# Weight-quarter differences moved from GpSimd to VectorE, squaring moved to ScalarE, tiles placed at multiples of 512 bytes, in a two-layer encoder on one core

## The chip, the cores and the metric

The kernel runs on one core of one Trainium2 chip. The metric is device time in microseconds (us) of one execution. The median of a few runs is compared, before and after the change, on the same chip. One further execution was recorded by the hardware profiler; all rows below are of it. Engine names follow the profile: PE is TensorE's matmul, PEld its weight load, DVE is VectorE, ACT is ScalarE, POOL is GpSimd, SP is the queue that issues the DMAs.

## The reference, cut to what matters

Two layers over 512 tokens of 1024 channels, all in float32. A layer projects its input, runs three attention branches (A with 4 heads, B with 8 query heads, C with 4 heads), gates and merges them, projects, normalizes, and then runs an MLP:

```python
for layer in range(DEPTH):                     # DEPTH = 2
    h = x @ w_in[layer]                        # q, k, v of three branches, gate logits
    oa, ob, oc = ...                           # the three attentions, 512 x 512 scores a head
    merged = g0 * (oa @ w_branch_a) + g1 * (ob @ w_branch_b) + g2 * (oc @ w_branch_c)
    x = layer_norm(ALPHA * x + merged @ w_out[layer])
    ff = jnp.square(jax.nn.relu(x @ w_up[layer])) @ w_down[layer]   # 1024 -> 4096 -> 1024
    x = layer_norm(ALPHA * x + ff)
```

## The kernel before

**Products.** Each float32 operand is split into a high and a low part of the fast float32 format, and each product is three matmuls, high by high, high by low and low by high (`mm3`, lines 152 to 155). A weight tile of 128 x 1024 arrives by DMA as `raw` (or `braw`), ACT copies it into `whi` (line 182), and DVE subtracts to give `wlo` (line 183). Eight split tiles are in flight: five in the pool `wts`, three in a second weight pool that exists outside of attention. PE frees them one after another, and a tile that is freed lets the next split start.

**Stages of a layer.** Projections and three attentions run interleaved (matmuls into `psq`, `psc`, `psg`, `psb`, `pss`, `pso`, transposes into `psp`, `psk`); then a tail of branch B's gates (`psg`, 24 matmuls) and branch products (`psb`, 12 matmuls) for eight column blocks m; then the output projection with its layer norm, and the MLP. The MLP runs in four quarters q of 1024 hidden channels.

**A quarter of the MLP.** Eight blocks m go through PE into `psu` (24 matmuls each). After each block `hidden(m, ps)` runs: ACT takes Relu out of the bank into half of a tile `f` (line 910), DVE squares it in place (line 911), and the result is split into `hh` on ACT (line 231) and `hl` on DVE (line 232). In quarters 0 to 2 the down projection is a seven-product scheme for 2 x 2 blocks (the class `Fast`), so `hidden` also makes sums and differences of the squares: after an odd m, line 918 (`f[:,4] = f[:,0] + f[:,2]`) and line 921 (three differences), all on DVE, 128 x 256 each. Slot 0 of `hh` and `hl` is split after an even m, slots 1 to 3 and 4 to 6 after an odd m.

**A `Fast` pass.** Seven steps of 24 matmuls each into `psd`. The first step takes slot 0 of all four pairs of blocks, the pair of m = 6 and 7 last (matmuls 10 to 12 of the first bank). The weights of a step are a quarter of the down matrix or a difference of quarters. `operand(i, half)` makes it: six tiles `braw` are loaded for a pass and two more at step 5, and for four of the seven steps (i = 1, 2, 4, 6) a tile is overwritten by the difference of two, once for each half:

```python
if a is not None:
    nc.gpsimd.tensor_tensor(dst, a, b, op=ALU.subtract)      # line 796, 128 x 1024
```

That is 8 differences in a pass and 48 in the kernel. Each reads tiles that were split shortly before, and is split itself next.

**The first quarter of a layer** is cut in token halves for its first four blocks (line 925), so their four banks are done about 2.9 us apart, where the other blocks are 5.45 us apart. Quarter 3 uses a plain down projection without differences.

**Order.** A tile scheduler orders each engine's queue when the program is built. Within an engine, instructions run in that order, each waiting for its own semaphores.

**Placement.** Pools lie one behind the other in each partition's memory, and their tiles are multiples of 64 bytes. In the built program `raw`, `whi`, `wlo` of `wts`, `xTh` and `xTl` (the transposed input) start 192 bytes past a multiple of 512, the second weight pool 448 past, the tiles of attention 320 or 64 past (`oh` and `ol`, the attention outputs that `psb` multiplies: 320), and the MLP's tiles 192 past.

Of the kernel before, what the change touches and what calls it, by code (L numbers as in the profile page):

```python
# [11 lines left out]
F32 = mybir.dt.float32  # L12
F32R = mybir.dt.float32r
AF = mybir.ActivationFunctionType
ALU = mybir.AluOpType
AX = mybir.AxisListType

P = 128
# [4 lines left out]
KB = D // P  # L23
# [13 lines left out]
C_OFF = {0: 0, 1: 256, 2: 640, 3: 1024}  # L37
C_WID = 1280
LINE = 16


class Split:
# [86 lines left out]
def encoder(ctx: ExitStack, tc: tile.TileContext, x, x_t, w_qkv, w_c, w_gate, b_gate, qn, kn, rpb,  # L129
            w_ba, w_bb, w_bc, w_out, ln1_g, ln1_b, w_up, w_down, w_fast, ln2_g, ln2_b,  # L130
            mask_a, rope_a, rope_b, out):
    nc = tc.nc
    const = ctx.enter_context(tc.tile_pool(name="const", bufs=1))
# [1 line left out]
    glob = ctx.enter_context(tc.tile_pool(name="glob", bufs=1))  # L135
    dram = ctx.enter_context(tc.tile_pool(name="dram", bufs=1, space=bass.MemoryType.DRAM))
    edge = ctx.enter_context(tc.tile_pool(name="edge", bufs=1, side="right"))
    edge.tile([P, LINE // 2], F32, name="edge")
    psum = ctx.enter_context(tc.tile_pool(name="psum", bufs=8, space=bass.MemoryType.PSUM))

    def bank(name):
        return psum.tile([P, 512], F32, tag="ps", name=name)

    def f32(ap):
        return ap.bitcast(F32)

    ident = const.tile([P, P], F32, name="ident")
    make_identity(nc, ident)
    nhalf = const.tile([P, 16], F32, name="nhalf")
    nc.vector.memset(nhalf, -0.5)  # L150

    def mm3(ps, lhs, rhs, start, stop, again=False):
# [110 lines left out]
    def layer_norm(pool, z, st, gb, after=None):  # L263

        mv = pool.tile([P, LINE], F32, tag="mv", name="mv", bufs=4)[:, :2]
        nc.vector.bn_aggr(mv, st.rearrange("p a b -> p (a b)"))
        ve = pool.tile([P, LINE], F32, tag="ve", name="ve", bufs=4)[:, :2]
        nc.vector.tensor_scalar(ve[:, :1], mv[:, 1:2], LN_EPS, None, op0=ALU.add)
# [7 lines left out]
    def stats_tile(pool):  # L276
        return pool.tile([P, LINE], F32, tag="st", name="st", bufs=4)[:, :12].rearrange("p (a b) -> p a b", a=2)

# [19 lines left out]
    def attention(l, keep, qk, open_heads):  # L298
# [72 lines left out]
        def norm_rotate(tb):  # L371

            raw = raws["b"][:, tb]
            r = raw.rearrange("p (h d) -> p h d", d=HD)
            sq = pool.tile([P, 10, HD], F32, tag="sq", name="sq", bufs=2)
            nc.scalar.activation(sq, r, AF.Square)
            cs = pool.tile([P, 2, 2, HD], F32, tag="cs", name="cs", bufs=1)
            nc.vector.tensor_tensor(cs, gqk, ropeb[:, :, tb][:, None].to_broadcast([P, 2, 2, HD]), op=ALU.mult)
            yield 1
            ss = pool.tile([P, 2, LINE], F32, tag="ss", name="ss", bufs=2)[:, :, :10]  # L380
            nc.vector.tensor_reduce(ss[:, 0], sq, axis=AX.X, op=ALU.add)
            nc.vector.tensor_scalar(ss[:, 0], ss[:, 0], 1.0 / HD, RMS_EPS, op0=ALU.mult, op1=ALU.add)
            nc.gpsimd.tensor_tensor(ss[:, 1], ss[:, 0], nhalf[:, :10], op=ALU.pow)
            yield 2
            nc.vector.tensor_tensor(r, r, ss[:, 1][:, :, None].to_broadcast([P, 10, HD]), op=ALU.mult)
            t2 = pool.tile([P, 10, HD], F32, tag="sq", name="t2", bufs=2)
            spans = ((0, 8), (8, 10))
            for i, (h0, h1) in enumerate(spans):
                r4, t4 = (t[:, h0:h1].rearrange("p h (a b d) -> p h a b d", a=2, b=2) for t in (r, t2))
                sin = cs[:, i, 1].rearrange("p (a b d) -> p a b d", a=2, b=2)  # L390
                for b in range(2):
                    nc.gpsimd.tensor_tensor(t4[:, :, :, b], r4[:, :, :, 1 - b],
                                            sin[:, None, :, b].to_broadcast([P, h1 - h0, 2, 16]), op=ALU.mult)
            yield 2
            for i, (h0, h1) in enumerate(spans):
                nc.vector.tensor_tensor(r[:, h0:h1], r[:, h0:h1],
                                        cs[:, i, 0][:, None, :].to_broadcast([P, h1 - h0, HD]), op=ALU.mult)
            nc.vector.tensor_tensor(r, r, t2, op=ALU.add)
            if tb == TB - 1:
                flags.add("b")  # L400
# [106 lines left out]
        def keys_of(name, qb):  # L507
            return C_KEYS[qb] if name == "c" else (0, TB)

        def scores(name, h, qb):  # L510
            ks, qs = pairs[name, h // 2]
            q, k = qs[h % 2], ks[h % 2]
            k0, k1 = keys_of(name, qb)
            n = (k1 - k0) * P
            ps = bank("pss")[:, :n]
            nc.tensor.matmul(ps, q[:, qb * P:(qb + 1) * P], k.hi[:, k0 * P:k1 * P], start=True, stop=False)
            nc.tensor.matmul(ps, q[:, qb * P:(qb + 1) * P], k.lo[:, k0 * P:k1 * P], start=False, stop=True)
            p = pool.tile([P, S], F32, tag="p", name="p", bufs=4)[:, :n]
            st = pool.tile([P, LINE], F32, tag="stat", name="stat", bufs=4)
            if name == "b":  # L520
                s = ps
                nc.vector.tensor_reduce(st[:, 0:1], ps, axis=AX.X, op=ALU.max)
            else:
                s = p
                add = maska[:, (3 - qb) * P:(3 - qb) * P + S] if name == "a" else bias[h][:, C_OFF[qb]:C_OFF[qb] + n]
                nc.vector.tensor_tensor_reduce(s, ps, add, 1.0, -3e38, ALU.add, ALU.max, st[:, 0:1])
            nc.vector.tensor_scalar(st[:, 1:2], st[:, 0:1], -1.0, None, op0=ALU.mult)
            nc.scalar.activation(p, s, AF.Exp, bias=st[:, 1:2], accum_out=st[:, 2:3])

            def normalize():  # L530
                nc.vector.reciprocal(st[:, 3:4], st[:, 2:3])  # L531
                (nc.vector if name == "c" else nc.gpsimd).tensor_scalar(p, p, st[:, 3:4], 1.0, op0=ALU.mult, op1=ALU.mult)  # L532

            return p, normalize
# [115 lines left out]
        with tc.manual_schedule() if l == 0 else nullcontext():  # L650
            work.flush()
        pool = open_heads()
        hb = keep.tile([P, 4 * KB], F32, tag="hb", name="hb")[:, :3 * KB]
        nc.sync.dma_start(hb, b_gate[l])
        nc.vector.tensor_scalar(hb, hb, 0.5, None, op0=ALU.mult)
        gqk = pool.tile([P, 2, 2, HD], F32, tag="gqk", name="gqk", bufs=1)
# [108 lines left out]
    class Fast:  # L765
# [18 lines left out]
        def operand(self, i, half):  # L784

            if i == 0 and half == 0:
                for quarter in (0, 1, 3):
                    for h in range(2):
                        self.load(quarter, h, quarter)
            if i == 5:  # L790
                self.load(2, half, 1)
            b11, b12, b22 = (self.b[k, half] for k in (0, 1, 3))
            dst, a, b = ((b11, None, None), (b11, b12, b11), (b11, b22, b11), (b22, None, None),
                         (b12, b22, b12), (b12, None, None), (b11, b12, b11))[i]
            if a is not None:
                nc.gpsimd.tensor_tensor(dst, a, b, op=ALU.subtract)  # L796
            return dst

        def items(self):
# [37 lines left out]
    for l in range(L):  # L837
        with ExitStack() as left:
            def pool(stack, name, side="left"):
                return stack.enter_context(tc.tile_pool(name=f"{name}{l}", bufs=1, side=side, reuse_waits="tile"))  # L840

            keep = pool(left, "keep")
            with ExitStack() as inner:
                def open_heads():
                    right.close()
                    return pool(inner, "heads")
# [15 lines left out]
            with ExitStack() as inner:  # L862
# [12 lines left out]
                st = [stats_tile(mix) for _ in range(TB)]  # L875
# [22 lines left out]
            for q in range(4):  # L898
                hid, sums = [], []

                def hidden(m, ps):

                    if m % 2 == 0:
                        hid.append(mlp.tile([P, 8, 256], F32, tag="f", name="f"))
                        sums.append(Split(mlp.tile([P, 7, 256], F32R, tag=f"hh{m}", name="hh"),
                                          mlp.tile([P, 7, 256], F32R, tag=f"hl{m}", name="hl")))
                    f, h = hid[-1], sums[-1]
                    a = 2 * (m % 2)
                    r = f[:, a:a + 2]
                    nc.scalar.activation(r, ps.rearrange("p (a n) -> p a n", a=2), AF.Relu)  # L910
                    nc.vector.tensor_tensor(r, r, r, op=ALU.mult)
                    if q == 3:
                        split_psum(h.map(lambda t: t[:, a:a + 2]), r)
                    elif a == 0:
                        split_psum(h.map(lambda t: t[:, 0]), f[:, 1])
                    else:

                        nc.vector.tensor_tensor(f[:, 4], f[:, 0], f[:, 2], op=ALU.add)  # L918
                        split_psum(h.map(lambda t: t[:, 1:4]), f[:, 2:5])
                        for dst, x1, x2 in ((5, 4, 1), (6, 1, 0), (7, 3, 5)):  # L920
                            nc.vector.tensor_tensor(f[:, dst], f[:, x1], f[:, x2], op=ALU.subtract)
                        split_psum(h.map(lambda t: t[:, 4:7]), f[:, 5:8])
# [25 lines left out]
                st = [stats_tile(mlp) for _ in range(TB)]  # L948
# [133 lines left out]
```

## Time and profile before

| | us |
|---|---|
| median of 3 runs (lowest, highest) | 1533.81 (1532.96, 1535.28) |
| the profiled execution | 1538.57 |
| its span, first to last instruction | 1536.8 |
| PE busy | 1501.1 |
| DVE busy | 1096.1 |
| ACT busy | 688.0 |
| POOL busy | 311.6 |

Busy times are sums over the span of the profiled execution. A matmul's record is longer than the step from one matmul to the next, since matmuls are pipelined: for speed, the starts of successive matmuls are to be compared. In a timeline row, the columns are the start, the length, engine, line, operation, output and inputs with their shape, and the count; brackets hold the idle time of the engine just before and what ended it. Overlapping neighbours on one engine by up to 0.1 us are its pipeline.

### The profile page before, as it was taken

The page shows a single profiled execution, that of the slowest core. Times are in us where ns is not written, and L with a number is a line of the kernel's source. Part 1 is how long each engine was busy: PE and PEld are TensorE (multiplying, and loading weights), DVE is VectorE, ACT ScalarE, POOL GpSimd, SP SyncE. Part 2 cuts the span into 40 slices and gives each one's busy share as a digit, 9 for nine tenths or more (in the row PEclk, how much of TensorE's full clock was granted, in tenths as well). Part 3 has the DMA queues.
Part 4 walks back from the last instruction along what each step waited for, and adds up shares of the span by engine and source line. Part 5 has one row for each costly group of instructions (what it writes and reads, how often), then busy time and mean ns, then how long its engine had stood idle before and what let it go on. Part 6 is the DMA issues. An engine that isn't in the chain of part 4 may idle for free.

```text
span 1536.8 us, 19258 instructions
## 1 busy us (share of the span) xinstructions
PE 1501.1 (98%) x7256; PEld 1255.7 (82%) x7256; DVE 1096.1 (71%) x1722; ACT 688.0 (45%) x1096; POOL 311.6 (20%) x238
## 2 busy tenths in 40 slices
PE   7999999999998999999999999999999989999997
PEld 6888888888896888888888888888888968888886
DVE  4677977745588797964666787876447888979636
ACT  4565656533134343433236556565332343535320
POOL 0112212311142222210101141233111413222001
PEclk9999999999998999999999999999999999999999
DMA  6222321143242415042331323112441342340411
GB/s 218 84 79 70 112 68 53 58 164 118 75 178 81 139 56 164 1 131 85 114 129 56 99 77 110 55 55 76 160 133 56 152 137 83 91 129 28 138 55 55
DMA packets 43438, 150.63 MB, mean 98 GB/s; under 512 B 5073, under 2 KB 5713, under 8 KB 43345
## 3 DMA queue, kind: packets, MB, share of 16 engines
q1 hardware_dynamic: 43344, 149.40, 30.8%
q8 instruction: 57, 0.93, 0.2%
q14 instruction: 37, 0.30, 0.1%
HBM read 145.19 MB, written 4.19 MB: 97 GB/s over the span
## 4 chain that ended last, share of the span: by engine, by line
PE 88%; DVE 7%; ACT 2%; issue 1%; DMA 1%; POOL 0%; SPq 0%; POOLq 0%; DVEq 0%; ACTq 0%
PE psd L153 8%; PE psd L154 8%; PE psd L155 8%; PE psu L154 6%; PE psu L153 6%; PE psu L155 6%; PE psg L155 6%; PE psg L154 6%; PE psg L153 6%; PE psp L547 3%; PE psq L153 2%; PE psq L155 2%; PE psq L154 2%; DVE wlo L183 2%; PE psb L155 2%; PE psb L153 2%
## 5 line engine op out<-in xcount | busy, mean ns | idle before, releaser
L183 DVE TENSOR_TENSOR wlo<-raw,whi 128x1024 fp32r<-128x1024 f32 (+1 forms) x198 | 247.9, 1253 | 204.2 <-ACT whi L182 201.9
L182 ACT ACTIVATE whi<-raw 128x1024 fp32r<-128x1024 f32 (+1 forms) x198 | 207.7, 1051 | 268.7 <-DMA raw<-in_w_up 110.6
L153 PE MATMUL psu<-xTh,whi 128*128 128x512 f32 (+1 forms) x576 | 210.8, 366 | 0.0
L154 PE MATMUL psu<-xTl,whi 128*128 128x512 f32 (+1 forms) x576 | 210.7, 366 | 0.0
L155 PE MATMUL psu<-xTh,wlo 128*128 128x512 f32 (+1 forms) x576 | 210.4, 365 | 0.0
L153 PE MATMUL psd<-whi,hh 128*128 128x512 f32 x464 | 183.2, 395 | 14.8 <-ACT hh L231 14.8
L796 POOL TENSOR_TENSOR braw<-braw 128x1024 f32<-128x1024 f32 x48 | 130.1, 2713 | 332.7 <-DVE wlo L183 169.2
L154 PE MATMUL psd<-wlo,hh 128*128 128x512 f32 x464 | 182.3, 393 | 0.0
L155 PE MATMUL psd<-whi,hl 128*128 128x512 f32 x464 | 182.2, 393 | 0.0
L153 PE MATMUL psg<-xTh,whi 128*128 128x512 f32 x384 | 156.7, 408 | 0.0
L155 PE MATMUL psg<-xTh,wlo 128*128 128x512 f32 x384 | 151.6, 395 | 0.0
L154 PE MATMUL psg<-xTl,whi 128*128 128x512 f32 x384 | 151.5, 395 | 0.0
L532 POOL TENSOR_SCALAR p<-p,stat 128x512 f32<-128x512 f32 x96 | 70.4, 734 | 361.5 <-DVE stat L531 247.1
L183 DVE TENSOR_TENSOR wlo<-braw,whi 128x1024 fp32r<-128x1024 f32 x84 | 126.7, 1508 | 18.3 <-ACT whi L182 16.7
L231 ACT ACTIVATE hh<-f 128x768 fp32r<-128x768 f32 (+2 forms) x88 | 60.8, 691 | 144.8 <-DVE f L918 79.4
L153 PEld LDWEIGHTS psu<-xTh,whi 128*128 128x128 f32 x576 | 108.6, 189 | 17.5
L154 PEld LDWEIGHTS psu<-xTl,whi 128*128 128x128 f32 x576 | 108.6, 189 | 17.5
L155 PEld LDWEIGHTS psu<-xTh,wlo 128*128 128x128 f32 x576 | 108.6, 189 | 17.5
L153 PEld LDWEIGHTS psd<-whi,hh 128*128 128x128 f32 x464 | 88.3, 190 | 34.8 <-ACT hh L231 16.5
L182 ACT ACTIVATE whi<-braw 128x1024 fp32r<-128x1024 f32 x84 | 87.9, 1051 | 47.9 <-DMA braw<-in_w_fast 25.3
L155 PEld LDWEIGHTS psd<-whi,hl 128*128 128x128 f32 x464 | 88.1, 190 | 18.9 <-DVE hl L232 0.5
L154 PEld LDWEIGHTS psd<-wlo,hh 128*128 128x128 f32 x464 | 88.3, 190 | 18.3
(121 smaller groups left out, 2991.3 us busy)
## 6 DMA issues: line engine op xcount, KB each, us to landing
raw<-in_w_up SPq DMA_DIRECT2D x64, 512.0 KB, 3.7
raw<-in_w_gate SPq DMA_DIRECT2D x48, 512.0 KB, 3.6
braw<-in_w_fast SPq DMA_DIRECT2D x48, 512.0 KB, 3.7
raw<-in_w_qkv SPq DMA_DIRECT2D x22, 512.0 KB, 3.6
raw<-in_w_out SPq DMA_DIRECT2D x16, 512.0 KB, 3.5
raw<-in_w_down SPq DMA_DIRECT2D x16, 512.0 KB, 3.5
raw<-in_w_c SPq DMA_DIRECT2D x12, 512.0 KB, 3.6
bias<-in_rpb SPq DMA_DIRECT2D x8, 640.0 KB, 4.0
```

The lines of the kernel that those rows point to most:

```text
L153: nc.tensor.matmul(ps, lhs.hi, rhs.hi, start=start, stop=False, skip_group_check=again)
L154: nc.tensor.matmul(ps, lhs.hi, rhs.lo, start=False, stop=False, skip_group_check=again)
L155: nc.tensor.matmul(ps, lhs.lo, rhs.hi, start=False, stop=stop, skip_group_check=again)
L182: nc.scalar.activation(hi[:, s], raw[:, s], AF.Copy)
L183: nc.vector.tensor_tensor(lo[:, s], raw[:, s], f32(hi[:, s]), op=ALU.subtract)
L231: nc.scalar.activation(dst.hi, ps, AF.Copy)
L532: (nc.vector if name == "c" else nc.gpsimd).tensor_scalar(p, p, st[:, 3:4], 1.0, op0=ALU.mult, op1=ALU.mult)
L547: nc.tensor.transpose(ps[:, j * P:(j + 1) * P], p[:, j * P:(j + 1) * P], ident)
L796: nc.gpsimd.tensor_tensor(dst, a, b, op=ALU.subtract)
```

## The change

It does three things. The difference of two weight quarters is issued on VectorE. The square in `hidden` is an ACTIVATE with the function Square on ScalarE, in place, behind the Relu on the same engine. And paddings are added to the pools, so that tiles start at multiples of 512 bytes.

```diff
+ROW = 128
...
-    edge.tile([P, LINE // 2], F32, name="edge")
+    edge.tile([P, ROW - LINE // 2], F32, name="edge")
...
+    const.tile([P, 3 * ROW // 4], F32, name="pad")
...
-    nhalf = const.tile([P, 16], F32, name="nhalf")
+    nhalf = const.tile([P, ROW], F32, name="nhalf")[:, :16]
...
-            ss = pool.tile([P, 2, LINE], F32, tag="ss", name="ss", bufs=2)[:, :, :10]
+            ss = pool.tile([P, 2, ROW // 2], F32, tag="ss", name="ss", bufs=2)[:, :, :10]
...
-            st = pool.tile([P, LINE], F32, tag="stat", name="stat", bufs=4)
+            st = pool.tile([P, ROW], F32, tag="stat", name="stat", bufs=4)
...
-        hb = keep.tile([P, 4 * KB], F32, tag="hb", name="hb")[:, :3 * KB]
+        hb = keep.tile([P, ROW], F32, tag="hb", name="hb")[:, :3 * KB]
...
-                nc.gpsimd.tensor_tensor(dst, a, b, op=ALU.subtract)
+                nc.vector.tensor_tensor(dst, a, b, op=ALU.subtract)
...
-                    nc.vector.tensor_tensor(r, r, r, op=ALU.mult)
+                    nc.scalar.activation(r, r, AF.Square)
```

Lines of the changed kernel are two higher from line 148 on. In its built program all tiles named above start at multiples of 512, but for the output projection's pool (`mh`, `ml`), which starts 256 past. PE's and SP's queues hold the same instructions in the same order as before. DVE's, ACT's and POOL's differ in the MLP alone.

DVE's queue in the first quarter of layer 0, before: from the square of block m = 1 on. `f` with the number 4104 belongs to blocks 0 and 1, 4169 to blocks 2 and 3; `braw` 4252 and 4254 are the two halves of one quarter of the weights.

```order
L183 TENSOR_TENSOR wlo_4376<-braw_4254,whi_4375 128x1024
L911 TENSOR_TENSOR f_4104<-f_4104 128x512
L918 TENSOR_TENSOR f_4104<-f_4104 128x256
L921 TENSOR_TENSOR f_4104<-f_4104 128x256 x2
L183 TENSOR_TENSOR wlo_4381<-braw_4252,whi_4380 128x1024
L232 TENSOR_TENSOR hl_4106<-f_4104,hh_4105 128x768 x2
L183 TENSOR_TENSOR wlo_4414<-braw_4254,whi_4413 128x1024
L911 TENSOR_TENSOR f_4169<-f_4169 128x512 x2
L232 TENSOR_TENSOR hl_4171<-f_4169,hh_4170 128x256
```

DVE's queue at the same place now (numbers are one higher):

```order
L185 TENSOR_TENSOR wlo_4377<-braw_4255,whi_4376 128x1024
L920 TENSOR_TENSOR f_4105<-f_4105 128x256
L798 TENSOR_TENSOR braw_4255<-braw_4259,braw_4255 128x1024
L923 TENSOR_TENSOR f_4105<-f_4105 128x256
L234 TENSOR_TENSOR hl_4107<-f_4105,hh_4106 128x768
L923 TENSOR_TENSOR f_4105<-f_4105 128x256
L185 TENSOR_TENSOR wlo_4382<-braw_4253,whi_4381 128x1024
L185 TENSOR_TENSOR wlo_4415<-braw_4255,whi_4414 128x1024
L234 TENSOR_TENSOR hl_4107<-f_4105,hh_4106 128x768
L798 TENSOR_TENSOR braw_4253<-braw_4261,braw_4253 128x1024
L798 TENSOR_TENSOR braw_4255<-braw_4263,braw_4255 128x1024
L234 TENSOR_TENSOR hl_4172<-f_4170,hh_4171 128x256
```

The squares (line 911) have left, and differences (line 798) stand between the splits; six of a pass's eight differences stand ahead of the `hl` of block m = 6.

ACT's queue at the end of the same quarter, before: blocks 6 and 7 are `f` 4328, blocks 4 and 5 are 4241.

```order
L231 ACTIVATE hh_4242<-f_4241 128x768 x2
L182 ACTIVATE whi_4454<-braw_4260 128x1024
L910 ACTIVATE f_4328<-psu_4303 128x512
L231 ACTIVATE hh_4329<-f_4328 128x256
L182 ACTIVATE whi_4485<-braw_4262 128x1024
L910 ACTIVATE f_4328<-psu_4340 128x512
L231 ACTIVATE hh_4329<-f_4328 128x768
```

And now:

```order
L233 ACTIVATE hh_4243<-f_4242 128x768 x2
L184 ACTIVATE whi_4455<-braw_4261 128x1024
L912 ACTIVATE f_4329<-psu_4304 128x512
L913 ACTIVATE f_4329<-f_4329 128x512
L233 ACTIVATE hh_4330<-f_4329 128x256
L184 ACTIVATE whi_4486<-braw_4263 128x1024
L912 ACTIVATE f_4329<-psu_4341 128x512
L913 ACTIVATE f_4329<-f_4329 128x512
L233 ACTIVATE hh_4330<-f_4329 128x768
```

Each square (line 913) stands behind its Relu, ahead of the `hh` that needs it.

## Rows read from the trace of the kernel before

**Rows 1.** The page: busy time by engine, share of the span, instructions.

```profile
PE 1501.1 (98%) x7256; PEld 1255.7 (82%) x7256; DVE 1096.1 (71%) x1722; ACT 688.0 (45%) x1096; POOL 311.6 (20%) x238
```

**Rows 2.** The waits: who waited for whom, us in total, times, longest.

```profile
ACT hh L231 <- DVE f L918: 79.4, 24, 6.4
...
PE psd L153 <- ACT hh L231: 14.8, 3, 7.4
```

**Rows 3.** Busy time by stretch: first and second `Fast` pass of layer 0, of layer 1.

```profile
core 0: us, PE busy (x) PEld busy (x) DVE busy (x) ACT busy (x) POOL busy (x), PEclk, DMA share, GB/s
470.34:518.51 48.17, 41.10 (x169) 33.42 (x168) 37.78 (x46) 21.35 (x24) 5.45 (x2) 0.89 0.47 141
562.03:600.40 38.37, 38.37 (x171) 31.79 (x170) 29.84 (x35) 16.06 (x17) 5.73 (x2) 1.00 0.55 167
1229.70:1277.26 47.56, 40.20 (x169) 32.72 (x168) 37.46 (x45) 21.16 (x25) 4.80 (x2) 0.93 0.45 139
1320.78:1359.14 38.36, 38.36 (x169) 31.38 (x168) 30.00 (x34) 16.11 (x18) 5.71 (x2) 1.00 0.53 164
```

**Rows 4.** Timeline of PE where the first `Fast` pass of layer 0 stops.

```profile
472.15 0.39 PE L155 MATMUL psd<-whi,hl 128*128 128x512 f32 x1
479.61 0.80 PE L153 MATMUL psd<-whi,hh 128*128 128x512 f32 x1 [7.07 <-ACT hh L231]
```

**Rows 5.** Timeline of DVE in the first quarter of layer 0's MLP.

```profile
444.01 2.71 DVE L183 TENSOR_TENSOR wlo<-braw,whi 128x1024 fp32r<-128x1024 f32 x1 [0.65 <-ACT whi L182]
...
447.36 2.51 DVE L918 TENSOR_TENSOR f<-f 128x256 f32<-128x256 f32 x1
449.90 2.97 DVE L921 TENSOR_TENSOR f<-f 128x256 f32<-128x256 f32 x2
...
453.92 4.02 DVE L232 TENSOR_TENSOR hl<-f,hh 128x768 fp32r<-128x768 f32 x2
457.86 3.42 DVE L183 TENSOR_TENSOR wlo<-braw,whi 128x1024 fp32r<-128x1024 f32 x1
461.20 3.49 DVE L911 TENSOR_TENSOR f<-f 128x512 f32<-128x512 f32 x2
...
464.95 0.41 DVE L918 TENSOR_TENSOR f<-f 128x256 f32<-128x256 f32 x1
...
467.28 1.22 DVE L183 TENSOR_TENSOR wlo<-braw,whi 128x1024 fp32r<-128x1024 f32 x1
468.41 0.95 DVE L232 TENSOR_TENSOR hl<-f,hh 128x768 fp32r<-128x768 f32 x1
470.09 0.69 DVE L911 TENSOR_TENSOR f<-f 128x512 f32<-128x512 f32 x1 [0.72 <-ACT f L910]
...
479.59 0.43 DVE L232 TENSOR_TENSOR hl<-f,hh 128x256 fp32r<-128x256 f32 x1
```

**Rows 6.** Groups by line: the differences on POOL, all 48.

```profile
L796 POOL TENSOR_TENSOR braw<-braw 128x1024 f32<-128x1024 f32 x48 | 130.1, 2713 | 332.7 <-DVE wlo L183 169.2 <-DMA braw<-in_w_fast 162.8
```

**Rows 7.** Timeline of POOL in the same stretch.

```profile
446.80 5.32 POOL L796 TENSOR_TENSOR braw<-braw 128x1024 f32<-128x1024 f32 x2 [1.17 <-DVE wlo L183]
454.08 6.11 POOL L796 TENSOR_TENSOR braw<-braw 128x1024 f32<-128x1024 f32 x2 [1.96 <-DVE wlo L183]
461.36 2.78 POOL L796 TENSOR_TENSOR braw<-braw 128x1024 f32<-128x1024 f32 x1 [1.16 <-DVE wlo L183]
```

**Rows 8.** Groups by shape: an ACTIVATE from memory to memory of the square's size.

```profile
L231 ACT ACTIVATE hh<-f 128x512 fp32r<-128x512 f32 x16 | 10.1, 633 | 19.9 <-DVE f L911 19.9
```

**Rows 9.** Timeline of PE in the tail: twelve `psb`, then twenty-four `psg`.

```profile
334.36 0.40 PE L153 MATMUL psb<-oh,whi 128*128 128x512 f32 x1
...
337.15 0.39 PE L153 MATMUL psg<-xTh,whi 128*128 128x512 f32 x1
...
340.34 0.39 PE L155 MATMUL psg<-xTh,wlo 128*128 128x512 f32 x1
...
342.61 0.40 PE L153 MATMUL psb<-oh,whi 128*128 128x512 f32 x1
```

## Prediction

> **What bounds the kernel now.** The page comes first: PE is busy for 1501.1 of 1536.8 us [rows 1]. With 98% it is the bound nearly everywhere, and no change on DVE, ACT or POOL can give back more than the time in which PE stands still or runs at the lower clock. So the second view is the waits, for rows in which PE is the one that waits. There is one of size: PE waited three times, 14.8 us in all, for ACT's `hh` [rows 2]. ACT had itself waited 79.4 us for DVE's sums of squares [rows 2].
>
> The third view is the busy time by stretch. The first `Fast` pass of each layer takes 48.17 and 47.56 us, the second passes, with the same 168 matmuls, 38.37 and 38.36 us [rows 3]. In the two longer ones PE's granted clock has a mean of 0.89 and 0.93, in the others 1.00: after the idle time a part of the matmuls runs at 1.2 GHz and not at 2.4. The timeline shows where they stop: nine matmuls into the step and a half of a bank, PE waits from 472.4 to 479.61 for the `hh` of the last pair, blocks 6 and 7 [rows 4].
>
> Why is that `hh` late? DVE's timeline of the quarter shows the same operations at two prices [rows 5]. Between 444 and 465 us a split of 128 x 1024 takes 2.71 and 3.42 us, a sum of 128 x 256 2.51, two `hl` of 128 x 768 4.02 together, two squares 3.49. From 465 us on they take 1.22, 0.41, 0.95 each and 0.69 each. The long ones lie beside POOL's differences, 2.7 us each, of which five are shown here [rows 6, 7]; when the last of them ends, at 464.14, the lengths are back to normal. A DVE operation with two inputs in memory that meets such a difference lasts until the difference is over.
>
> **The change part by part.**
>
> *Differences to DVE.* 48 of them leave POOL [rows 6]. On DVE each is a subtraction of 128 x 1024 with two inputs in memory, the same shape as `wlo`, so 1.22 us [rows 5]; upper bound the 2.71 that the same shape took beside POOL, which no longer applies, since no POOL work of size is left in the MLP. Six of them come ahead of the `hl` of block 6: 7.4 us.
>
> *What DVE gets back.* In this quarter, from rows 5, actual less undisturbed: 1.49 + 2.20 for the two splits, 2.10 for the sum, 2.97 - 0.82 = 2.15 for the two differences of squares, 4.02 - 1.90 = 2.12 for the `hl`, 3.49 - 1.38 = 2.11 for the squares: 12.2 us.
>
> *Squares to ACT.* Seven squares (blocks 0 to 6) no longer stand on DVE ahead of that `hl`: 7 x 0.69 = 4.8 us. On ACT each costs about what `hh` of the same 128 x 512 costs, 0.633 us [rows 8], so 4.4 us up to there and 8 x 0.63 = 5.1 us a quarter. ACT was busy for 21.35 of 48.17 us in the pass [rows 3], and its long waits in the quarter ended on DVE [rows 2], so this is hidden. It also removes a handover to DVE and back between Relu and `hh`.
>
> *Net on the late `hh`.* The `hl` of block 6 ended at 480.0 [rows 5]. By the three terms it ends 12.2 + 4.8 - 7.4 = 9.6 us earlier, at 470.4. It is needed at 472.8, two matmuls after the `hh` at 472.4 (nine steps of 227 ns after the start of the pass at 470.34). Followed forward from the first Relu, with the new order and these prices, I get 469 to 470. So the wait is gone with 2 to 3 us to spare. What is late next: the sums of blocks 6 and 7, of which slot 3 is needed by the second step at 477.8; block 7 leaves PE at 470.34, and Relu, square, one sum, `hh` and `hl`, with two splits between, end at about 475.5. Then the supply of weights: DVE was busy for 29.84 us in an undisturbed pass of 38.37 [rows 3]; the new one has fewer long operations and two differences (2.4 us), so it keeps up. Only the differences that stand ahead on DVE's queue could hold it: a difference waits for the landing of its quarter and for ACT's copy of the tile that it overwrites, and behind it `hl` and `wlo` are queued. The third difference, which reads the tile loaded last, was under way on POOL by 452.1 [rows 7]; DVE comes to it at about 452, so no landing holds it.
>
> *The sum of this part.* Both first passes then take what the second ones take: 48.17 - 38.37 = 9.8 and 47.56 - 38.36 = 9.2, together 19.0 us [rows 3]. This contains the idle time and the stretch at 1.2 GHz behind it, which needs the idle time. Other quarters had no wait of size on PE; what DVE gains there lies beside PE and is worth nothing. The pow of the layer norm on POOL stays.
>
> *Placement.* No row shows a tile at a multiple of 512, so this is bounded. In the tail, twelve `psb` take 337.15 - 334.36 = 2.79 us, 232 ns each; in the `psg` that follow, the last ten take 2.27 us, 227 ns each, as in the MLP (38.37 us for 168 matmuls) [rows 3, 9]. The `psg` multiply two tiles that lie 192 past a multiple of 512, the `psb` one at 192 or 448 and one at 320: their offsets differ by an odd multiple of 128. Whether that is the cause, no row tells. If it is, the change makes all of them alike. The lower end is 0; the upper end is 7 ns for each of the about 2,000 matmuls of 512 columns in attention and the tails (from the loops), 14 us. The first `psg` behind a `psb` also take 233 ns until the rhythm is back, and that follows any switch of shape, which placement does not remove. I take 4 us: about 2 for the 384 `psb` at 5.5 ns, and 2 for the rest, nearer to the low end. In the MLP every matmul already has the good rhythm, in both weight pools, so 0 there.
>
> The Trainium skill, on the page "TensorE: Matmul & The Clock Gate", section "Wait — 56ns, not 53.3ns?", states that back-to-back matmuls of 512 columns start 215.7 ns apart at the full clock; the rows here say 227 [rows 9]. By the page there would be 11 ns in each matmul that something in this kernel adds.
>
> **Sum.** 19.0 + 4 = 23.0 us. The profiled execution would go from 1538.57 (span 1536.8) to 1515.6. The median of the runs stands 4.8 us under the profiled execution; the same difference gives 1533.8 - 23.0 = 1510.8, so 1511 us. From 1500 (placement worth 14) to 1516 (placement worth nothing, a wait of 1 us left) for this case by itself.
>
> **The rivals.**
>
> *Half of the wait stays.* DVE is a single queue, and six differences now stand in it where POOL had its own. If one of them waits 3 to 5 us for a landing or a copy, the `hl` of blocks 4 to 6 are late by as much and PE stands still again, with a stretch at 1.2 GHz behind. For it: margins of only 2 to 3 us. Against it: prices and readiness above. With half of 19 us and little from placement: 1522 to 1525.
>
> *Nothing moves.* The wait that ends last is another, such as ACT's queue, now longer by the squares, in which `hh` of blocks 4 and 5 stand ahead. Then about 1534. Against it: ACT waited for DVE, not the reverse [rows 2].
>
> *Placement speeds up every matmul.* The distance itself from a multiple of 512 may cost each matmul something, in the MLP too. With the only price that rows show for a placement, 5.5 ns, on all of some 5,700 matmuls of 512 columns: 31 us, and with the 19 us 1484. Against it: `psg` in the tail reads weights at 192 and the MLP at 192 and at 448 with the same 227, so the distance shows no effect. By the page's 215.7 it would be 11 ns each, 63 us, and about 1452.
>
> *Slower: placement brings all matmuls to the price of `psb`.* If two tiles read at the same time disturb each other when both stand at one fixed place, as weights and inputs at 0 now do, then the 5,700 matmuls go from 227 to 232 or 233 ns: 5,700 x 5.5 = 31 us lost, less 19 gained, 1546. It decides from 3.3 ns a matmul on. Against it: weights and inputs stood at the same offset, 192, before, and gave the good rhythm [rows 3, 9].
>
> **How the numbers follow.** Forecast, both waits gone: 0.74. Half stays: 0.12. Nothing moves: 0.05. Every matmul faster: 0.03. Slower: 0.06. The predicted time is the forecast's, 1511. To leave no more than 2 in 10 out, the range takes the forecast's 1500 to 1516 (0.72) and most of the half case (0.09): 1500 to 1525. About 0.2% (3 us) is what a measurement of this kernel can tell from no change; faster by more: 0.74 + 0.12 + 0.03 = 0.89; within: 0.05; slower: 0.06.
>
> **What would show it.** Right: both first `Fast` passes at 38.4 us with a clock of 1.00; no wait of PE for `hh` over 1 us; sums of 128 x 256 at 0.42 us everywhere; differences at 1.22 us on DVE; squares at 0.6 us on ACT; twelve `psb` in 2.72 us if placement counts, 2.79 if not. Wrong: a stretch of the MLP in which PE waits for DVE behind a difference; starts of MLP matmuls that are not 227 ns apart.

## The result and the profile after

| | before | after |
|---|---|---|
| median of 4 runs, us (lowest, highest) | 1534.55 (1532.96, 1537.35) | 1513.33 (1510.30, 1513.81) |
| the profiled execution, us | 1538.57 | 1513.81 |

The ratio of the times is 0.9856, with a 95% interval from 0.9836 to 0.9875: faster by 21.2 us, and by 24.8 us between the two profiled executions. The forecast was 1511 us, from 1500 to 1525.

The busy line of the changed kernel's page, to be held against [rows 1]: POOL has lost 130 us, DVE 78, and ACT has 41 more.

```profile
PE 1491.7 (99%) x7256; PEld 1252.4 (83%) x7256; DVE 1018.2 (67%) x1706; ACT 729.3 (48%) x1160; POOL 181.1 (12%) x190
```

Waits of PE in the changed kernel (who waited for whom, us in total, times, longest). These are all of them; the row of 14.8 us for `hh` in [rows 2] is gone. ACT's own waits for DVE ahead of `hh` have gone from 143.7 us to 20.8 (11.6 + 9.2). The groups below have them behind the last bar, the kernel before first; the 143.7 are the sums (79.4) and differences of squares (14.8) and the squares (29.6, and 19.9 in [rows 8]).

```profile
PE psq L155 <- ACT whi L184: 6.5, 1, 6.5
PE psp L549 <- POOL p L534: 4.6, 2, 2.3
PE psq L155 <- ACT xTh L827: 1.0, 1, 1.0
```

```profile
L231 ACT ACTIVATE hh<-f 128x768 fp32r<-128x768 f32 x48 | 40.6, 847 | 95.0 <-DVE f L918 79.4 <-DVE f L921 14.8
...
L231 ACT ACTIVATE hh<-f 128x256 fp32r<-128x256 f32 x24 | 10.0, 418 | 29.8 <-DVE f L911 29.6
```

```profile
L233 ACT ACTIVATE hh<-f 128x768 fp32r<-128x768 f32 x48 | 40.3, 843 | 21.1 <-DVE f L923 11.6 <-DVE f L920 9.2
```

Busy time by stretch of the changed kernel, first and second `Fast` pass of layer 0, then of layer 1, with the columns of [rows 3]. Each stretch begins with the first matmul of the pass. The first passes now last 38.08 us where they lasted 48.17 and 47.56, the granted clock is 1.00, and POOL does nothing.

```profile
467.90:505.98 38.08, 38.08 (x170) 31.54 (x169) 28.56 (x33) 16.36 (x17) 0.00 (x0) 1.00 0.57 172
549.50:587.80 38.30, 38.30 (x170) 31.73 (x169) 28.59 (x34) 16.36 (x17) 0.00 (x0) 1.00 0.53 165
1215.37:1253.45 38.08, 38.08 (x170) 31.53 (x168) 28.72 (x33) 16.37 (x17) 0.00 (x0) 1.00 0.58 179
1296.97:1335.05 38.08, 38.08 (x170) 31.53 (x168) 28.75 (x33) 16.36 (x17) 0.00 (x0) 1.00 0.54 166
```

Groups by line and shape of the changed kernel: the differences on DVE, the squares on ACT, and the two lines of sums and differences of squares (busy us, mean ns). The sums of 128 x 256 had means of 1290 (line 918 before) and 828 ns (line 921 before); now they take 424 and 422 ns, the undisturbed length.

```profile
L798 DVE TENSOR_TENSOR braw<-braw 128x1024 f32<-128x1024 f32 x48 | 58.2, 1219 | 3.9 <-DMA braw<-in_w_fast 3.9
...
L923 DVE TENSOR_TENSOR f<-f 128x256 f32<-128x256 f32 x72 | 30.0, 422 | 2.7 <-ACT f L913 2.1
...
L920 DVE TENSOR_TENSOR f<-f 128x256 f32<-128x256 f32 x24 | 10.2, 424 | 0.0
```

```profile
L913 ACT ACTIVATE f<-f 128x512 f32<-128x512 f32 x64 | 40.3, 632 | 1.8
```

The `hl` of block 6 in the first quarter, on DVE's timeline (start, length):

```profile
466.19 0.42 DVE L234 TENSOR_TENSOR hl<-f,hh 128x256 fp32r<-128x256 f32 x1
```

It ends at 466.61. Its matmul is the twelfth of the pass, 2.49 us (eleven steps) after the start at 467.90, so at 470.39: 3.8 us to spare. In the kernel before it ended at 480.0, 7.2 us late.

**Where the 24.8 us lie.** PE's order is the same in both kernels, so the start of one and the same matmul can be compared in both. From the start of the first `Fast` pass of each layer to that of its last matmul's successor: 10.09 and 9.49 us; two smaller stops in the second and third pass of layer 1: 0.28 and 0.69 us. That is 20.55 us of waits. Attention with its tails: 3.35 us, shown below. The opening, before 71 us: 0.90 us.

### The profile page after: what moved, and what is told of

Read it like the earlier page. It is cut to its first block, busy times and chain, and to the rows that moved or that the text cites. A ratio compares the mean times of both kernels' runs of the same rounds, so it can differ in the third digit from the quotient of the medians.

```text
span 1511.9 us, 19202 instructions
## 1 busy us (share of the span) xinstructions
PE 1491.7 (99%) x7256; PEld 1252.4 (83%) x7256; DVE 1018.2 (67%) x1706; ACT 729.3 (48%) x1160; POOL 181.1 (12%) x190
## 4 chain that ended last, share of the span: by engine, by line
PE 95%; DVE 2%; DMA 1%; ACT 1%; issue 0%; POOL 0%; SPq 0%; POOLq 0%; DVEq 0%; ACTq 0%
PE psd L157 9%; PE psd L156 9%; PE psd L155 9%; PE psu L156 8%; PE psu L157 8%; PE psu L155 8%; PE psg L157 6%; PE psg L156 6%; PE psg L155 6%; PE psp L549 3%; PE psq L155 2%; PE psq L157 2%; PE psq L156 2%; PE psb L156 2%; PE psb L155 2%; PE psb L157 2%
## 5 line engine op out<-in xcount | busy, mean ns | idle before, releaser
L185 DVE TENSOR_TENSOR wlo<-braw,whi 128x1024 fp32r<-128x1024 f32 x84 | 102.5, 1223 | 50.4 <-ACT whi L184 49.0
L271 POOL TENSOR_TENSOR ve<-ve,nhalf 128x1 f32<-128x1 f32 x16 | 24.1, 1507 | 742.7 <-DVE ve L270 742.7
L155 PE MATMUL psq<-whi,xTh 128*128 128x512 f32 (+1 forms) x256 | 90.0, 352 | 7.5 <-ACT whi L184 6.5
```

The source lines that it names most:

```text
L155: nc.tensor.matmul(ps, lhs.hi, rhs.hi, start=start, stop=False, skip_group_check=again)
L185: nc.vector.tensor_tensor(lo[:, s], raw[:, s], f32(hi[:, s]), op=ALU.subtract)
L271: nc.gpsimd.tensor_tensor(ve[:, 1:], ve[:, :1], nhalf[:, :1], op=ALU.pow)
```

## The experiments

The theory: POOL's long differences make DVE's operations last until they are over, so `hh` and `hl` of blocks 6 and 7 come late; and tiles of one matmul an odd multiple of 128 bytes apart cost some 6 ns a matmul. The rivals: the detour of the squares over DVE is the cause of the wait; the placement does more, or nothing.

**Differences alone.** One line of the kernel before:

```diff
-                nc.gpsimd.tensor_tensor(dst, a, b, op=ALU.subtract)
+                nc.vector.tensor_tensor(dst, a, b, op=ALU.subtract)
```

> The kernel before with the differences alone moved to DVE; squares stay on DVE, tiles stay where they were. Theory (POOL's long differences lengthen DVE's two-input operations, and that alone makes the `hh` of blocks 6 and 7 late): the `hl` of block 6 ends at 480.0 - 12.2 + 7.4 = 475.2 by the rows of the kernel before, 2.4 us after PE needs it; by the changed kernel, where it ended 6 us ahead of its use, less 4.8 us for the squares, it is in time. So a wait of 0 to 2.4 us in place of 7.2, and 1515 to 1523 us. Sums of 128 x 256 take 0.42 us everywhere. Rival (the squares' detour over DVE is the cause, the differences are not): DVE only has 7.4 us more to do, the wait of 7 us stays or grows, 1534 to 1540 us.

Measured: 1515.57 us, ratio 0.9869 (0.9856 to 0.9882), 20.2 us less than the 1535.78 beside it. The first passes of the two layers, and the `hl` of block 6 on DVE's timeline:

```profile
470.51:508.68 38.17, 38.17 (x169) 31.45 (x168) 30.44 (x37) 15.84 (x17) 0.00 (x0) 1.00 0.55 165
1218.33:1256.51 38.18, 38.18 (x169) 31.46 (x168) 29.64 (x37) 15.72 (x17) 0.00 (x0) 1.00 0.55 166
```

```profile
472.72 0.42 DVE L232 TENSOR_TENSOR hl<-f,hh 128x256 fp32r<-128x256 f32 x1
```

It ends at 473.14 and is needed at 470.51 + 2.49 = 473.00. So it is late by 0.1 us, and the pass lasts 0.1 us longer than the 38.08 of the changed kernel. The rival falls: the differences are the cause. The 6 us of margin in the expectation were misread, from an `hl` of block 5; 3.8 was right, and 3.8 - 4.8 = -1.0 would have been the sum.

**Squares alone.** The other line:

```diff
-                    nc.vector.tensor_tensor(r, r, r, op=ALU.mult)
+                    nc.scalar.activation(r, r, AF.Square)
```

> The kernel before with the squares alone moved to ACT; the differences stay on POOL. Theory (long POOL differences are the cause): DVE's operations keep their two prices; the squares take at most 4.8 us out of its queue, so the `hl` of block 6 ends at about 475.2 and PE still waits 2 to 3 us in each layer with a stretch at 1.2 GHz behind: 1520 to 1526 us. Rival (the detour of the squares is the cause): no wait is left, 1514 to 1517 us. Second rival (DVE merely waits longer beside POOL, so that the 4.8 us are lost again): 1532 to 1535 us.

Measured: 1526.26 us (1520.57 to 1528.37), ratio 0.9931 (0.9915 to 0.9947), 9.5 us less: 0.3 above the 1520 to 1526 expected, and outside of what both rivals expected. PE's wait, the two first passes, and DVE's timeline in the first quarter of layer 0:

```profile
PE psd L153 <- ACT hh L231: 6.3, 2, 3.1
```

```profile
466.46:510.71 44.25, 41.11 (x169) 33.42 (x168) 32.55 (x39) 20.91 (x24) 5.33 (x2) 0.92 0.50 152
1221.79:1264.88 43.09, 39.98 (x169) 32.52 (x168) 33.78 (x39) 20.77 (x24) 5.44 (x2) 0.96 0.51 156
```

```profile
443.44 5.05 DVE L921 TENSOR_TENSOR f<-f 128x256 f32<-128x256 f32 x2
448.41 3.17 DVE L232 TENSOR_TENSOR hl<-f,hh 128x768 fp32r<-128x768 f32 x1
...
460.06 0.87 DVE L921 TENSOR_TENSOR f<-f 128x256 f32<-128x256 f32 x2
...
471.79 0.43 DVE L232 TENSOR_TENSOR hl<-f,hh 128x256 fp32r<-128x256 f32 x1
```

The long operations are still there (two differences of squares in 5.05 us, and in 0.87 where POOL is idle), and PE waits 3.1 us a layer. The clock of 0.92 and 0.96 shows the stretch at 1.2 GHz behind the wait. The squares alone take about half of the wait out. So each edit alone brings much, and together they bring less than their sum. By the starts of the same matmuls, in the first `Fast` passes alone: 19.4 us by the differences, 8.4 by the squares, 19.6 by both. (The medians, 20.2, 9.5 and 23.4 us, hold the openings as well, see below.) Behind the differences the squares are worth 0.2 us in the passes (38.17 and 38.18 to 38.08).

**Placement alone**, the seven lines of the change that only pad or widen tiles.

> The kernel before with the new places of tiles alone; differences on POOL and squares on DVE. Theory: attention and its tails save what the two traces differ by there, 1.8 + 0.6 us in layer 0 and 1.2 + 0.7 us in layer 1, so 4 us: 1530 us, with both waits for `hh` of about 7 us still there. Rival (placement has no effect, the 4 us came from other timing): 1534 us. Second rival (placement is behind the lengths of DVE's operations too): 1513 to 1517 us.

Measured: 1532.52 us. The median is 3.3 us less than the 1535.78 beside it; by the ratio, 0.9976 (0.9967 to 0.9984), it is 3.7 us, from 2.5 to 5.1. PE's wait for `hh` is as before:

```profile
PE psd L155 <- ACT hh L233: 15.0, 3, 7.4
```

**Differences and squares, no placement.** Both lines of the first two.

> The kernel before with differences on DVE and squares on ACT, tiles where they were. Theory: both waits gone, 19 to 20 us less than before, 1514 to 1516 us; the twelve `psb` of the tail still take 2.79 us. Rival (placement carries more than 4 us): 1520 us or more. Second rival (placement is worth nothing): the same as the changed kernel, 1513 us.

Measured: 1512.38 us, ratio 0.9850 (0.9837 to 0.9863), below the 1514 to 1516 expected. By the times alone this is the changed kernel, 1513.33 and, in five more runs of it, 1511.98, as the second rival said. By the trace it isn't: its twelve `psb` take 2.79 us, its attention and tail 246.97 and 57.73 as in the kernel before. What makes up for that is the opening. Two stretches of each, from the start to the matmul ahead of PE's first wait for `p`, and on from there to one and the same `pso`; the changed kernel first, then this one:

```profile
0.00:50.46 50.46, 42.94 (x218) 35.96 (x219) 28.46 (x54) 25.27 (x38) 0.69 (x6) 1.00 0.58 189
50.46:70.00 19.54, 17.23 (x85) 14.23 (x84) 11.18 (x31) 10.22 (x21) 5.12 (x6) 0.91 0.27 81
```

```profile
0.00:48.81 48.81, 40.80 (x219) 34.39 (x219) 27.99 (x54) 25.17 (x38) 0.69 (x6) 1.00 0.61 196
48.81:66.80 17.99, 15.72 (x86) 13.04 (x85) 11.05 (x31) 10.09 (x21) 5.12 (x6) 1.00 0.28 89
```

The wait for `p` is the same in both (2.3 us), but in one the clock falls to 1.2 GHz behind it (0.91) and in the other it stays (1.00). This and the opening ahead of it make 3.2 us, and the first wait for `p` in layer 1, with the clock again falling in the changed kernel alone, makes 1.6 more. So the changed kernel lost 4.8 us there and gained 3.4 by placement, and its profile is 1.6 us longer. In the profiles of the fourteen runs of this study that same `pso` starts either between 66.8 and 67.4 us (two of these four have another wait for `p`, see the last experiments) or between 68.7 and 71.1. Is it the placement that makes the clock fall? In the twelve profiles that leave these waits as they were it fell behind 16 of 24. Behind the one of layer 1 it fell in the kernel before and in the changed one, and stayed with placement alone and with both lines alone, so either placement shows both. How often each does, so few profiles can't tell. The two medians therefore cannot show what the placement adds; it is read from the stretches behind.

**Where the tiles stand.** Three kernels put `oh` and the heads' tiles elsewhere. The first is the kernel before with one line of the change, which moves them from 320 to 192 bytes past a multiple of 512, where weights and inputs stand. The two others are the changed kernel with that line at another size (`[P, 32]` and `[P, 64]`), which puts them at 128 and at 256 and leaves weights and inputs at 0.

```diff
-        hb = keep.tile([P, 4 * KB], F32, tag="hb", name="hb")[:, :3 * KB]
+        hb = keep.tile([P, 128], F32, tag="hb", name="hb")[:, :3 * KB]
```

> The kernel before with one line of the change, the wider tile for `hb`: it shifts `oh` and the heads' tiles from 320 to 192 past a multiple of 512, where weights and inputs stand; nothing but the small constants stands at a multiple of 512. Theory (what costs is two tiles of one matmul that stand an odd multiple of 128 bytes apart): the twelve `psb` of the tail take 2.72 us (227 ns each) in place of 2.79, and attention and tails save about 3.6 us as in the changed kernel. Rival (multiples of 512 themselves count): 2.79 us, nothing saved. The waits for `hh` stay, so the time is 1530 to 1532 by the theory, 1534 to 1536 by the rival.

> The changed kernel with the old, narrow tile for `hb`: `oh` and the heads' tiles stand at 128, all else at 0. Theory (an odd multiple of 128 bytes between the two tiles costs): the twelve `psb` of the tail take 2.79 us again and the 3.6 us of placement are lost: 1514 to 1517. Rival (only places that are no multiple of 128 cost): 2.72 us and 1510 to 1514.

> The changed kernel with a tile for `hb` of 256 bytes: `oh` and the heads' tiles stand at 256, all else at 0. Theory (odd multiples of 128 between the two tiles cost, 256 does not): the twelve `psb` of a tail step take 2.72 us, and attention as in the changed kernel. Rival (only the same place in 512 bytes is good): 2.79 us, and 3.6 us lost.

Attention of layer 0 behind its opening, and the tail up to the last of its eight `psb` groups, by busy time in the stretch; in this order the kernel before, the changed one, all at 192, `oh` at 128, and `oh` at 256:

```profile
70.91:317.87 246.96, 246.96 (x1264) 206.86 (x1263) 188.97 (x418) 148.63 (x295) 62.96 (x70) 1.00 0.25 77
317.87:375.59 57.72, 57.72 (x253) 47.30 (x252) 25.60 (x26) 19.98 (x25) 9.02 (x7) 1.00 0.41 135
```

```profile
70.00:315.93 245.93, 245.93 (x1264) 206.68 (x1262) 188.90 (x418) 148.62 (x295) 62.63 (x70) 1.00 0.25 77
315.93:373.05 57.12, 57.12 (x254) 47.30 (x252) 25.59 (x26) 19.98 (x25) 8.99 (x7) 1.00 0.42 136
```

```profile
69.79:315.45 245.66, 245.66 (x1264) 206.60 (x1262) 188.81 (x418) 148.73 (x295) 63.14 (x70) 1.00 0.25 77
315.45:372.57 57.12, 57.12 (x254) 47.31 (x252) 25.58 (x26) 20.00 (x25) 9.01 (x7) 1.00 0.42 138
```

```profile
70.28:317.11 246.83, 246.83 (x1263) 206.90 (x1262) 188.97 (x418) 148.67 (x295) 62.95 (x70) 1.00 0.25 77
317.11:374.84 57.73, 57.73 (x254) 47.29 (x252) 25.56 (x26) 20.01 (x25) 9.02 (x7) 1.00 0.41 135
```

```profile
69.69:315.62 245.93, 245.93 (x1263) 206.68 (x1262) 188.89 (x418) 148.86 (x295) 63.13 (x70) 1.00 0.25 78
315.62:372.74 57.12, 57.12 (x253) 47.30 (x252) 25.56 (x26) 20.00 (x25) 9.00 (x7) 1.00 0.43 135
```

The tail has two values and no third: 57.12 where the two tiles of a `psb` stand 0 or 256 bytes apart within 512, 57.73 where they stand 128 apart. The twelve `psb` of a tail step go with it, 2.72 and 2.79 us, in all fourteen profiles, and attention of layer 0 follows (245.7 to 246.0, or 246.8 to 247.0). Multiples of 512 have no part in it: with all at 192 the kernel has the same gain from one line (246.96 to 245.66 and 57.72 to 57.12). What the single line brings in all is 1531.71 us in its one run, by the trace 3.9 us in the two layers, where the seven bring 3.4: no less than the seven. (The expectations put the latter at 3.6.) The kernel with `oh` at 128 took 1515.67, the one at 256 1513.22, a run each; their traces carry the verdict. What smaller distances than 128 do was not tried, except that 64 bytes past (192) is as good as 0 where both tiles stand there.

**Any work on POOL?** The changed kernel with 20 operations on a small tile of their own on POOL, begun with the first square of a quarter (quarters 0 to 2):

```diff
+            idle = mlp.tile([P, 3 * ROW], F32, name="idle")
+            nc.vector.memset(idle, 0.0)
...
+                    if m == 0 and q < 3:
+                        nc.gpsimd.tensor_copy(idle[:, :1], r[:, 0, :1])
+                        for _ in range(20):
+                            nc.gpsimd.tensor_tensor(idle, idle, idle, op=ALU.subtract)
```

> The changed kernel with 20 subtractions of 128 x 384 on POOL in each of the first three quarters, begun at the first square of the quarter, on a small tile that nothing else reads: two inputs in memory, about 1.0 us each by the 2.71 us of 128 x 1024, so 20 us. No engine needs a result of them. Theory (a two-input operation on POOL holds up the two-input operations on DVE, whatever they compute): beside them a sum of 128 x 256 takes up to 1.4 us in place of 0.42, DVE gets late by 10 to 16 us against a margin of 6, PE waits for `hh` or `hl` at the start of the first seven-product pass again, and the time is 1518 to 1540 us. Rival (the differences were slow for another reason, such as what they read): DVE's lengths do not change, 1510 to 1514 us.

The second kernel has an operation of one input in its place, `nc.gpsimd.tensor_scalar(idle, idle, 1.0, 1.0, ...)`.

> The same with operations of one input on POOL (a multiplication by a constant, 128 x 384, about 0.5 us each by the 0.69 us of 128 x 512 in attention). Theory (two inputs on POOL's side are what holds DVE up): DVE's lengths stay at 0.42 and 1.22, PE does not wait, 1510 to 1514 us. Rival (any POOL operation holds DVE up): sums of 128 x 256 take 0.9 us beside them; the 10 us of POOL work make DVE at most 8 us late, with 6 us of margin, 1512 to 1518 us.

Measured: 1543.31 us with two inputs, 1521.83 us with one, a run each. PE's wait for `hh`, POOL's and DVE's timelines with two inputs, then with one:

```profile
PE psd L155 <- ACT hh L233: 23.7, 8, 6.6
...
440.60 26.74 POOL L919 TENSOR_TENSOR idle<-idle 128x384 f32<-128x384 f32 x20
...
445.24 1.04 DVE L926 TENSOR_TENSOR f<-f 128x256 f32<-128x256 f32 x1
446.20 1.84 DVE L798 TENSOR_TENSOR braw<-braw 128x1024 f32<-128x1024 f32 x1
```

```profile
PE psd L155 <- ACT hh L233: 4.5, 2, 2.3
...
440.39 20.26 POOL L919 TENSOR_SCALAR idle<-idle 128x384 f32<-128x384 f32 x20
...
444.04 0.72 DVE L926 TENSOR_TENSOR f<-f 128x256 f32<-128x256 f32 x1
444.68 1.52 DVE L798 TENSOR_TENSOR braw<-braw 128x1024 f32<-128x1024 f32 x1
```

A sum that lasts 0.42 alone lasts 1.04 or 0.72, a difference of 1.22 lasts 1.84 or 1.52: each of these DVE operations is longer by the same amount whatever its length, 0.62 beside the two-input work and 0.30 beside the one-input work. That is taking turns: each waits until the POOL operation under way is over. My expectation that one input on POOL is harmless fell; its rival was right in kind (0.72, where it said 0.9), and PE waited again. No engine needs what POOL computes here, so the turns are the cause that is left. Both times lie above what was expected, up to 1540 and, by the rival, up to 1518, which went by the misread margin of 6 us. In the first kernel the first passes last 49.65 and 49.57 us, later passes of both layers some 2 us more; in the second the first passes last 42.25 us.

```profile
467.90:517.55 49.65, 41.22 (x169) 33.23 (x168) 37.94 (x47) 24.03 (x29) 0.00 (x0) 0.90 0.45 138
```

Not every DVE operation takes part. In the kernel before, this one began while a difference was under way on POOL (492.58 to 495.63) and lasted what it lasts anywhere; one of its inputs, `psd`, is in PSUM, the memory that PE writes its sums to. All six that began beside a difference in that trace took 0.67 or 0.68 us:

```profile
493.29 0.68 DVE L259 SCALAR_TENSOR_TENSOR x<-x,psd 128x512 f32<-128x512 f32 x1
```

```profile
492.58 3.05 POOL L796 TENSOR_TENSOR braw<-braw 128x1024 f32<-128x1024 f32 x1 [0.29 <-DMA braw<-in_w_fast]
```

Nor does DVE's side need two inputs. In the kernel of the last experiment a division on DVE, with one input in memory and one factor a row, lasts 0.48 us. The two that began some 0.6 us into a POOL operation of 1.29 us lasted 0.94, to just past its end:

```profile
231.62 0.94 DVE L534 TENSOR_SCALAR p<-p,stat 128x512 f32<-128x512 f32 x1
```

A sum along the rows on DVE (`ss`, one input) took 0.80 to 0.81 us beside POOL, as it does alone. So not every form with one input takes part, and which do was not tried.

The Trainium skill, "SBUF — State Buffer", section "SBUF: two separate sides", has this as a rule: VectorE and GpSimd share a pair of ports; a VectorE operation with two inputs in SBUF and a GpSimd operation that reads SBUF both need it, and whichever begins first holds it for the whole instruction. The lengths above agree with it, also in that one input on POOL is enough.

**What is left, and a faster kernel.** PE's largest waits behind the first weights are the two for POOL's `p`. In the changed kernel the first division of scores on POOL is held up by a split of weights on DVE that began 0.07 us earlier; most of the others take 0.7 us:

```profile
51.34 1.22 DVE L185 TENSOR_TENSOR wlo<-raw,whi 128x1024 fp32r<-128x1024 f32 x1
...
51.41 1.70 POOL L534 TENSOR_SCALAR p<-p,stat 128x512 f32<-128x512 f32 x1 [50.12 <-DVE stat L529]
```

So the division of the first head goes to DVE:

```diff
-                (nc.vector if name == "c" else nc.gpsimd).tensor_scalar(p, p, ...)
+                (nc.vector if name == "c" or (name == "a" and h == 0) else nc.gpsimd).tensor_scalar(p, p, ...)
```

> The changed kernel with the division of the first head's scores (branch a, head 0) on DVE instead of POOL. PE's largest waits left are two of 2.3 us for POOL's `p` (the first of three divisions on POOL, begun at 51.41, lasted 1.71 us beside a DVE split of 1.22 that began at 51.34; alone one lasts 0.69). On DVE it follows the reciprocal at once: `p` is ready some 1.2 to 1.5 us earlier, twice. Theory: 2.5 to 3 us less than the changed kernel beside it, and up to 3.4 more where the stretch at 1.2 GHz goes as well. Rival (DVE's queue then holds the split of the weights up and PE waits for `wlo` instead): no difference, within 1 us.

> The changed kernel again, to have more of its times: 1510 to 1514 us, the lower end where no stretch at 1.2 GHz follows the first wait for `p` in a layer.

Measured: 1507.01 us, ratio 0.9811 (0.9798 to 0.9824); the changed kernel beside it 1511.98, ratio 0.9844 (0.9828 to 0.9861). So 5.0 us less. PE's waits and the first transposes on PE's timeline:

```profile
PE psp L549 <- DVE p L534: 1.7, 2, 1.0
```

```profile
52.17 0.41 PE L549 MATMUL psp<-ident,p 128*128 128x128 f32 x2 [0.97 <-DVE p L534]
```

2.9 us come from the two waits (4.6 to 1.7); the rest is put down to the clock, which in its profile no longer falls behind them. In layer 1 that stretch is 3.2 us shorter than in the profile of the changed kernel, 1.6 by the wait and 1.6 by the clock. The last kernel moves all 96 divisions:

> The changed kernel with all 96 divisions of scores that POOL does in attention moved to DVE. On POOL they last 0.735 us each, 70 us in all; with one input in memory and the lengths of the run before, DVE takes some 0.4 us each, 38 us more over two layers. Theory (in attention PE waits for POOL only at the first head of a layer, and DVE has room beside it): the gain of the run with head 0 alone and no more, 1506 to 1509 us. Rival (POOL's divisions hold up DVE's operations in attention, and that holds up PE): less than 1505 us. Second rival (DVE's one queue gets too long there): PE waits for `p`, 1510 us or more.

Measured: 1507.05 us, ratio 0.9820 (0.9806 to 0.9833), the same as with one head (behind the opening the two traces differ by 0.2 us). DVE has room in attention, and POOL's divisions cost PE nothing there but at the first head.

## Why the prediction was right, point by point

- **The bound and the late `hh`.** Right. The wait and the stretch at 1.2 GHz are gone, and the differences alone do it.
- **19.0 us for the two first passes.** 10.1 + 9.5 = 19.6. My measure for an undisturbed pass, 38.37, held the starts of a matmul or two too many; the pass lasts 38.08. Two smaller stops, in later passes of layer 1, brought 1.0 us that I had not looked for. The run with all tiles at 192 lost 0.9 of these as well, with its differences still on POOL, so the change need not be what removed them.
- **Prices.** Differences 1.22 us on DVE (1.219 measured), squares 0.633 on ACT (0.632), sums 0.42 everywhere: right. DVE is busy for 28.6 us of a first pass, so the supply of weights keeps up.
- **The margin.** Forecast: 2 to 3 us to spare; measured 3.8. The terms were less exact than their sum. Counted from the start of the pass, the differences alone brought the `hl` of block 6 forward by 7.0 us (480.0 to 473.14, in a pass that began 0.17 later), where 12.2 - 7.4 = 4.8 was worked out. The squares alone brought 3.9 (472.22, in a pass that began 3.88 earlier, so 476.1), where it was 4.8; that a part of it is lost beside POOL in the next turn is my guess. Together they brought 11.0, where it was 9.6. The two errors are of opposite sign, so the sum came out better than its terms deserved.
- **The mechanism as I put it** was too narrow on both sides. I spoke of DVE operations with two inputs in memory and of POOL's differences. POOL work with one input holds DVE up as well (+0.30 us), and a DVE division with one input is held up too (0.94 for 0.48). An operation with one of its two inputs in PSUM took no part, as my words would have it.
- **Placement, 4 us.** 3.4 us by the stretches (1.03 + 0.60 in layer 0, 1.11 + 0.61 in layer 1), 3.3 to 3.7 by the times of that edit alone. The twelve `psb` of a tail step take 334.97 - 332.25 = 2.72 us where they took 2.79, and the fourteen matmuls from the first `psg` on take 3.17 for 3.19 [rows 9]:

```profile
332.25 0.39 PE L155 MATMUL psb<-oh,whi 128*128 128x512 f32 x1
...
334.97 0.39 PE L155 MATMUL psg<-xTh,whi 128*128 128x512 f32 x1
...
338.14 0.39 PE L157 MATMUL psg<-xTh,wlo 128*128 128x512 f32 x1
```

  The guess behind it, an odd multiple of 128 between the two tiles, is what the runs at 192, 128 and 256 show. One reading in it was wrong: the 233 ns of the first `psg` behind a `psb` were put down to a switch of shape, which placement would leave as it is. Both are 128 x 512, and the fourteen now take some 227 ns each, so the 233 too came from the placement. (At a real switch, from 256 to 512 columns in the MLP, the first five steps take 228 to 236 ns in both kernels.) The two rivals on every matmul fall: in the MLP the 168 matmuls of an undisturbed pass take 38.08 us, 226.7 ns each, in each of these placements. The 215.7 ns of the Trainium skill's page "TensorE: Matmul & The Clock Gate", section "Wait — 56ns, not 53.3ns?", appear in no stretch here; none of these placements closes that gap, and what does was not tried.
- **From the profile to the median.** This step was weak. The profiled execution went from 1538.57 to 1513.81, 1.8 us below the 1515.6 of the sum (passes 0.6 more than forecast, small stops 1.0, opening 0.9, placement 0.6 less); but I carried the 4.8 us between profile and median over as if they were fixed, and after the change they are 0.5. The opening, with its two lengths some 3 us apart, can make such a difference. The two errors go opposite ways, so it is partly luck that 1511 was off by no more than 2.3 us.

## What to carry to other kernels

Work moved to an idle engine is not free if that engine shares something with a busy one: look for one operation with two prices in DVE's timeline, and lay POOL's timeline beside it. When two edits attack one wait, price the second behind the first: here the squares were worth 8.4 us in the first passes alone and 0.2 us there behind the differences. For a few microseconds compare starts of the same matmul in both traces; medians were disturbed by as much from an opening that the edits compared did not touch.

## What the runs showed of the hardware

- DVE and POOL take turns operation by operation: +0.62 us on each DVE operation with two inputs in memory beside a 128 x 384 subtraction on POOL, +0.30 beside a multiplication by a constant. A DVE division with one input took 0.94 us for 0.48. An operation with an input in PSUM (0.68 us) and a sum along rows (0.81 us) were not longer.
- Two tiles of a matmul 128 bytes apart, modulo 256, cost 6 ns a matmul of 512 columns in `psb` (2.79 to 2.72 us for twelve); where both stand within 512 bytes doesn't matter (0, 192).
- Behind waits of 1.8 to 2.5 us for `p` the granted clock fell to 1.2 GHz for a stretch in 16 of 24 cases and stayed at 2.4 in the others (0.91 and 1.00 from the wait to the same `pso`), worth 1.6 us in layer 1.
